# The second FFN's output product by one level of Strassen's algorithm

## The chip, the cores and the metric

The kernel runs on one core of one Trainium2 chip. The metric is device time in microseconds (us) of one execution; the profile is one execution taken by the hardware profiler, and its times are counted from the start of its span.

## The reference

One layer on 512 tokens of width 1024: a SwiGLU FFN, a mixing part (a gated linear recurrence and a forgetting attention), and a second SwiGLU FFN, each with a modulated norm ahead and a gated residual behind. Only the second FFN matters here:

```
u = rms_norm(x, ffn2_norm_g) * (1 + sc3) + sh3
a, b = jnp.split(u @ w_in, 2, axis=-1)          # w_in: 1024 x 5632
x = x + 0.5 * g3 * ((jax.nn.silu(a) * b) @ w_out)   # w_out: 2816 x 1024
```

All tensors are float32.

## The kernel before

Every product in float32 is made of three matmuls on split operands (`mm3`, L108 to L110): each operand is the sum of a high part in the format fp32r and a low part of the same format, and high times high, low times high and high times low are summed in PSUM. A weight block comes by a DMA of 512 KB issued on SP into `raw` (3 buffers), ScalarE (ACT) copies it to the high part `wh` (L89), VectorE (DVE) subtracts to get the low part `wl` (L91); `wh` and `wl` have 4 buffers each.

The hidden width 2816 is 22 blocks of 128 rows. The input product of the second FFN (`ffn_in_halves` for the first two blocks, `ffn_in` for the others) keeps the hidden values h transposed, with 128 rows of h on the partitions and 512 tokens along the free dimension. `ffn_h` makes h of a block from its two PSUM banks (`g`): ACT's silu (L324), DVE's product (L325), then the split into `hh` (L326, ACT) and `hl` (L327, DVE).

The output product is `token_gemm`, called twice, for the left and the right 512 columns of the output: in each call the 22 blocks of `w_out` are loaded in pairs (`w_mov`), and for each of the 4 blocks of 128 tokens there is one PSUM bank, in which 22 x 3 matmuls are summed. The banks of the first call are those of pool `t`, of the second those of pool `g` (4 banks each, 8 in all). The last two pairs (`tail`) are taken token block by token block, so that `residual` can finish one bank while the next is summed: DVE scales it with the gate (L388), adds x (L390), SP stores it (L394). x stays in the tiles `x0` to `x7` all the time.

The order of the instructions on each engine is set by the framework's scheduler, from the program's order and from its own estimate of the times. The engines take their instructions in that order, and semaphores hold an instruction until its inputs and its buffer are there. The wait for a buffer is a wait for its last reader.

Of the kernel before, what the change touches and what calls it, by code (L numbers as in the profile page):

```python
# [11 lines left out]
F32 = mybir.dt.float32  # L12
F32R = mybir.dt.float32r
I32 = mybir.dt.int32
AF = mybir.ActivationFunctionType
# [5 lines left out]
P = 128  # L21
T = 512
NT = 4
D = 1024
NK = 8
FF = 2816
NJ = 22
# [16 lines left out]
MUL, ADD, SUB, MAX, MIN = ALU.mult, ALU.add, ALU.subtract, ALU.max, ALU.min  # L44


class Layer:
# [285 lines left out]
    def ffn_in(self, w_in, j0, hp, tp, extra=None):  # L333
        for j in range(j0, NJ):
            pa, pb = self.gbank(), self.gbank()
            self.gemm_stat(pa, self.w_stat(w_in, j * P), 0, T)
            self.gemm_stat(pb, self.w_stat(w_in, FF + j * P), 0, T)
            self.ffn_h(pa, pb, j, 0, T, hp, tp)
            self.lo_after = None
            if extra:  # L340
                extra(j)

    def ffn_in_halves(self, w_in, nj, hp, tp):

        wa = [self.w_stat(w_in, j * P) for j in range(nj)]
        wb = [self.w_stat(w_in, FF + j * P) for j in range(nj)]
        pp = [(self.gbank(), self.gbank()) for _ in range(nj)]
        for h in range(2):
            for j in range(nj):
                c0, c1 = h * 256, (h + 1) * 256  # L350
                self.gemm_stat(pp[j][0], wa[j], c0, c1)
                self.gemm_stat(pp[j][1], wb[j], c0, c1)
                self.ffn_h(pp[j][0], pp[j][1], j, c0, c1, hp, tp)

    def token_gemm(self, lhs, nk, w, half, done, tail=2, extra=None, last=None):

# [565 lines left out]
    def run(self):  # L922
        nc, tc, A = self.nc, self.tc, self.A
# [5 lines left out]
        self.ntmp, self.xn_tiles = 5, self.xn_start  # L929
        with tc.tile_pool(name="f1t", bufs=1) as tp:  # L930
            self.consts(tp)
            with tc.tile_pool(name="st", bufs=1) as st:
# [2 lines left out]
            with tc.tile_pool(name="f1h", bufs=1) as hp:  # L935
# [12 lines left out]
                lhs = lambda k: (self.hh[k], self.hl[k])  # L948
# [25 lines left out]
        with tc.tile_pool(name="gates", bufs=1) as mp:  # L974
            ws = [self.w_stat(w_mix, m * P) for m in range(4)]
            pp = [self.gbank() for _ in range(4)]
# [6 lines left out]
            for m in range(4, 8):  # L983
                ps = self.gbank()
# [5 lines left out]
        with tc.tile_pool(name="att", bufs=1) as ip:  # L990
# [60 lines left out]
        with tc.tile_pool(name="br", bufs=1) as bp:  # L1051
# [12 lines left out]
            for m in range(NK):  # L1064
                t = self.branch(m, 1, bp, None)
# [5 lines left out]
            lhs = lambda k: (self.mh[k], self.ml[k])  # L1071
# [5 lines left out]
            self.norm_half(1, bp, G3, sh3)  # L1077
        ys.close()

        self.ntmp = 5  # L1080
        with tc.tile_pool(name="f2t", bufs=1) as tp, tc.tile_pool(name="f2h", bufs=1) as hp:
            for k in range(NK):
                self.dump(f"u3_{k}", self.uh[k].bitcast(F32))
            self.h_tiles(hp)
            self.ffn_in_halves(A["ffn2_w_in"][0], 2, hp, tp)
            self.ffn_in(A["ffn2_w_in"][0], 2, hp, tp)
            lhs = lambda k: (self.hh[k], self.hl[k])
# [32 lines left out]
```

## Time and profile before

| | |
|---|---|
| time, median of 3 runs | 1366.77 us (1366.6 to 1367.23) |
| profiled execution: time, span | 1367.67 us, 1365.9 us |
| PE (TensorE) busy | 1344.3 us, 98% of the span, 6586 matmuls |
| DVE busy | 800.8 us, 59% |
| ACT busy | 561.2 us, 41% |
| POOL (GpSimd) busy | 46.0 us, 3% |
| DMA | 183.36 MB, mean 134 GB/s |
| granted TensorE clock, mean | 0.999 |

How to read the rows: a row of the timeline gives start, duration, engine, line of the kernel, operation, out<-in, and in brackets how long the engine had been idle and what released it. A row of the waits gives the waiting engine and line, the one waited for, the sum, the number and the longest of the waits. A row of the windows gives for a stretch its length and each engine's busy time with the number of instructions, then the granted clock, the DMA engines' share and GB/s. A matmul's duration in the trace is its latency; the next one starts earlier.

### The profile page before, as it was taken

To read this page: it belongs to the slowest core of one execution; us is meant where nothing else is said; L and a number is where in the kernel's file an instruction comes from. 1 tells how busy PE (TensorE), PEld (TensorE's weight loads), DVE (VectorE), ACT (ScalarE), POOL (GpSimd) and SP (SyncE) were. 2 spreads that over 40 slices of the span, in tenths; PEclk is the share of its full clock that TensorE was granted. 3 is DMA by queue.
4 is the path that set the end of the run, shared out by engine and by line. 5 is a ranking of instruction groups with operands and counts; after the bars stand their busy time and mean duration, and the time that the engine had idled before them with its cause. 6 is when DMAs were issued, how large, how long until landed. Compare 5 with 4: busy or idle time off the path is not lost.

```text
span 1365.9 us, 17443 instructions
## 1 busy us (share of the span) xinstructions
PE 1344.3 (98%) x6586; PEld 1126.1 (82%) x6586; DVE 800.8 (59%) x1476; ACT 561.2 (41%) x945; POOL 46.0 (3%) x71
## 2 busy tenths in 40 slices
PE   7999999999999999999999999999999999999998
PEld 6788887887888888888888888888798888888887
DVE  6866666656467777886786875456473333332232
ACT  4532333323236655465665675332262223222120
POOL 2000000000011101000000000012010000000000
PEclk9999999999999999999999999999999999999999
DMA  9676556666534424434252532464323333333230
GB/s 290 185 220 191 180 181 198 215 205 193 184 89 112 117 93 135 127 104 132 63 148 72 162 109 70 132 193 147 92 79 108 94 106 94 93 96 105 101 123 31
DMA packets 216456, 183.36 MB, mean 134 GB/s; under 512 B 10866, under 2 KB 182546, under 8 KB 216372
## 3 DMA queue, kind: packets, MB, share of 16 engines
q1 hardware_dynamic: 215892, 182.17, 44.6%
q8 instruction: 52, 0.85, 0.3%
q14 instruction: 32, 0.26, 0.1%
q0 software_dynamic: 416, 0.06, 0.0%
q10 hardware_dynamic: 64, 0.02, 0.0%
HBM read 172.18 MB, written 10.03 MB: 133 GB/s over the span
## 4 chain that ended last, share of the span: by engine, by line
PE 89%; DVE 6%; ACT 3%; DMA 1%; issue 1%; SPq 0%; DVEq 0%; ACTq 0%
PE g L110 23%; PE g L108 23%; PE g L109 23%; PE t L110 4%; PE t L109 4%; PE t L108 4%; PE g L510 2%; PE t L854 2%; PE t L824 1%; DVE wl L91 1%; PE t L795 1%; PE t L796 1%; PE t L510 1%; DVE fq L774 1%; DMA A<-A_d 1%
## 5 line engine op out<-in xcount | busy, mean ns | idle before, releaser
L91 DVE TENSOR_TENSOR wl<-raw,wh 128x1024 fp32r<-128x1024 f32 x214 | 269.4, 1260 | 272.6 <-ACT wh L89 255.7
L89 ACT ACTIVATE wh<-raw 128x1024 fp32r<-128x1024 f32 x214 | 225.8, 1060 | 493.7 <-PE g L109 150.8
L110 PE MATMUL g<-uh,wl 128*128 128x512 f32 (+2 forms) x984 | 369.7, 376 | 1.8 <-DVE wl L91 1.8
L108 PE MATMUL g<-uh,wh 128*128 128x512 f32 (+2 forms) x984 | 370.7, 377 | 0.0
L109 PE MATMUL g<-ul,wh 128*128 128x512 f32 (+2 forms) x984 | 369.7, 376 | 0.0
L110 PEld LDWEIGHTS g<-uh,wl 128*128 128x128 f32 (+1 forms) x984 | 184.7, 188 | 36.4 <-DVE wl L91 2.7
L109 PEld LDWEIGHTS g<-ul,wh 128*128 128x128 f32 (+1 forms) x984 | 184.9, 188 | 33.5
L108 PEld LDWEIGHTS g<-uh,wh 128*128 128x128 f32 (+1 forms) x984 | 184.8, 188 | 33.5 <-issue 0.6
L108 PE MATMUL g<-wh,uh 128*128 128x512 f32 (+1 forms) x320 | 111.8, 350 | 0.0
L110 PE MATMUL g<-wh,ul 128*128 128x512 f32 (+1 forms) x320 | 111.1, 347 | 0.0
L109 PE MATMUL g<-wl,uh 128*128 128x512 f32 (+1 forms) x320 | 110.9, 347 | 0.0
L325 DVE TENSOR_TENSOR sl<-g,sl 128x512 f32<-128x512 f32 (+1 forms) x45 | 29.9, 667 | 82.8 <-PE g L110 82.7
L284 DVE SCALAR_TENSOR_TENSOR acc<-raw,ccol,acc 128x1024 f32<-128x1024 f32 x49 | 62.9, 1283 | 14.5 <-DMA raw<-in_w_ada_dram 14.0
L108 PE MATMUL g<-wh,hh 128*128 128x512 f32 x176 | 69.2, 393 | 0.0
L110 PE MATMUL g<-wh,hl 128*128 128x512 f32 x176 | 69.1, 393 | 0.0
L108 PE MATMUL t<-wh,hh 128*128 128x512 f32 x176 | 69.1, 392 | 0.0
L110 PE MATMUL t<-wh,hl 128*128 128x512 f32 x176 | 69.1, 392 | 0.0
L109 PE MATMUL g<-wl,hh 128*128 128x512 f32 x176 | 69.0, 392 | 0.0
L109 PE MATMUL t<-wl,hh 128*128 128x512 f32 x176 | 69.0, 392 | 0.0
L108 PEld LDWEIGHTS g<-wh,uh 128*128 128x128 f32 x320 | 60.5, 189 | 7.8 <-DVE tk L709 0.5
L110 PEld LDWEIGHTS g<-wh,ul 128*128 128x128 f32 x320 | 60.5, 189 | 7.7
L109 PEld LDWEIGHTS g<-wl,uh 128*128 128x128 f32 x320 | 60.5, 189 | 7.4
(268 smaller groups left out, 1851.5 us busy)
## 6 DMA issues: line engine op xcount, KB each, us to landing
raw<-in_ffn_w_in_dram SPq DMA_DIRECT2D x82, 512.0 KB
raw<-in_w_ada_dram SPq DMA_DIRECT2D x56, 512.0 KB
raw<-in_w_mix_dram SPq DMA_DIRECT2D x48, 512.0 KB
raw<-in_ffn_w_out_dram SPq DMA_DIRECT2D x44, 512.0 KB
ar<-in_w_ada_dram SPq DMA_DIRECT2D x32, 256.0 KB
raw<-in_w_mix_dram SPq DMA_DIRECT2D x32, 256.0 KB
A<-A_d SPq DMA_DIRECT2D x16, 256.0 KB
raw<-in_w_branch_a_dram SPq DMA_DIRECT2D x8, 512.0 KB
```

The lines of the kernel that those rows point to most:

```text
L89: nc.scalar.activation(hi, src, AF.Copy)
L91: nc.vector.tensor_tensor(lo, src, hi, op=SUB)
L108: mm(ps, lh, rh, start=start, stop=False)
L109: mm(ps, lh, rl, start=False, stop=False)
L110: self.last_mm = mm(ps, ll, rh, start=False, stop=stop)
L284: nc.vector.scalar_tensor_tensor(acc, r, self.ccol[:, k:k + 1], acc, op0=MUL, op1=ADD)
L325: nc.vector.tensor_tensor(s[:, :w], ps_b[:, c0:c1], s[:, :w], op=MUL)
L510: mm = nc.tensor.matmul(acc_ps[b], (wl if p == 1 else wh)[:, b % 2, s], self.ul[k] if p == 2 else self.uh[k], start=k == 0 and p == 0, sto ...
L774: nc.vector.scalar_tensor_tensor(lo, b[own, :], gc[own, :], d[own, :], op0=MUL, op1=SUB)
L795: nc.tensor.matmul(ps[:, :w], q[:, s], k[:, :w], start=True, stop=False)
L796: nc.tensor.matmul(ps[:, :w], q[:, s], kl[:, :w], start=False, stop=True)
L854: nc.tensor.matmul(po[:, q0:], vt[:, kb, i, :], Px[:, o:o + T - q0], start=n == 1, stop=n == 8)
```

## The change

The output product is a 512 x 2816 by 2816 x 1024 product. Split in two in each direction, with the even and the odd blocks of h as the two halves of the inner dimension, it is eight products of half size (256 tokens, 11 blocks, 512 columns); Strassen's algorithm (in Winograd's form, with sums that are used again) makes it of seven, whose operands are sums and differences of the quarters of h and of `w_out`. The new function `pair_out` does it in two sweeps over `w_out`: the first sums three products in six banks (Z, X, Y for two token blocks each), 18 matmuls per pair of blocks; the second sums four (Z, Y, X, W) in eight banks, 24 matmuls per pair. A step is one pair; steps 0 to 10 of the second sweep are written 0' to 10' here.

- `pair_h` takes the place of `ffn_h`: the product silu(a) * b of an even block goes to `E`, of an odd one to `Ra`; when both are there, DVE makes the sums of the pair (L381, L382, L385, L386). The operands of the first sweep are split at once (ACT L383, DVE L384), the others stay unsplit in `Ra` and `Rb`. The first four pairs' `Ra` and `Rb` lie in the tiles of x; x is written to DRAM ahead of the second FFN (L1254, 8 stores of 256 KB) and read back in the second sweep.
- `pair_split` splits `Ra` and `Rb` of a pair: two copies on ACT (L405), two subtractions on DVE (L406).
- Per step of the first sweep, `load` fetches the two blocks of a pair (512 KB and 256 KB); DVE makes two differences of quarters of `w_out` (L440, L441), the split of the block of 1024 columns as before (L89, L91), and a split of one more half (L423 on ACT, L424 on DVE). The second difference is kept in `T2` for the second sweep.
- Between the sweeps the sums P1, U2, U4 leave the banks (ACT L452, DVE L454, L456).
- Per step of the second sweep, the two blocks are loaded again, POOL makes two differences (L473, L474), and three splits follow (L89 and L91; L479 and L480 twice).
- In steps 6' and 7' P1, U2 and U4 are scaled (DVE L463) and added to x on POOL (L465): six scalings and eight additions. The tail, steps 9' and 10', is taken bank by bank; the first six banks' additions to x are on POOL, the others on DVE.

```diff
-            self.ffn_h(pa, pb, j, 0, T, hp, tp)
+            self.ffn_act(pa, pb, j, 0, T, hp, tp)
...
+    def pair_h(self, ps_a, ps_b, j, c0, c1, hp, tp):
...
+        V(E[:, 1, :], E[:, 3, :], Ra[:, 1, :], op=ADD)
+        V(E[:, 2, :], E[:, 1, :], E[:, 0, :], op=SUB)
+        nc.scalar.activation(A1[:, 0:3, :], E[:, 0:3, :], AF.Copy)
+        V(A1[:, 3:6, :], E[:, 0:3, :], A1[:, 0:3, :], op=SUB)
+        V(Rb[:, 0, :], E[:, 0, :], E[:, 3, :], op=SUB)
+        V(Rb[:, 1, :], Ra[:, 0, :], E[:, 2, :], op=SUB)
...
+    def pair_split(self, i, hp, tp):
...
+        for n, R in enumerate((self.Ra[i], self.Rb[i])):
+            hi = A2[:, 2 * n:2 * n + 2, :]
+            nc.scalar.activation(hi, R, AF.Copy)
+            nc.vector.tensor_tensor(lo[n], R, hi, op=SUB)
...
+    def pair_out(self, w, v, hp, tp, x_src):
...
+        def load(r, c):
+            t = self.raw([P, 2, 512], [(lambda t: t, w[r * P:(r + 1) * P, :].rearrange("p (h n) -> p h n", h=2))])
+            o = tp.tile([P, 512], F32, name=self.nm("raw2"), tag="t2", bufs=self.ntmp)
+            nc.sync.dma_start(o, w[c * P:(c + 1) * P, 512:])
+            return t, o
+        for i in range(NP):
+            t, o = load(2 * i, 2 * i + 1)
...
+            V.tensor_tensor(t[:, 1, :], t[:, 1, :], t[:, 0, :], op=SUB)
+            V.tensor_tensor(T2[i], o, t[:, 1, :], op=SUB)
+            wh, wl = self.split(t, [P, 2, 512])
+            w2 = half(T2[i])
+            A1 = self.A1[i]
+            for ps, n, b in ((Z, 0, (wh[:, 0, :], wl[:, 0, :])), (X, 2, w2), (Y, 1, (wh[:, 1, :], wl[:, 1, :]))):
+                for tb in range(2):
+                    mm(ps, tb, (A1[:, n, :], A1[:, 3 + n, :]), b, i == 0, i == NP - 1)
+            if i % 2:
+                self.pair_split(i // 2, hp, tp)
...
+        def add(src, half, tbs, eng=V):
+            t = self.tmp(tp, "rs")
+            V.scalar_tensor_tensor(t, src, 0.5, g[half], op0=MUL, op1=MUL)
+            for tb in tbs:
+                eng.tensor_tensor(self.x[tb][half], self.x[tb][half], t, op=ADD)
...
+        def prepare(i):
+            if i >= NP // 2:
+                self.pair_split(i, hp, tp)
+            t, o = load(2 * i + 1, 2 * i)
+            G.tensor_tensor(o, t[:, 1, :], o, op=SUB)
+            G.tensor_tensor(T2[i], t[:, 0, :], T2[i], op=SUB)
+            wh, wl = self.split(t, [P, 2, 512])
...
+            for n, src in enumerate((o, T2[i])):
+                nc.scalar.activation(hi[:, n, :], src, AF.Copy)
+                V.tensor_tensor(lo[:, n, :], src, hi[:, n, :], op=SUB)
...
+        for i in range(NP - tail):
+            o = prepare(i)
+            for n in ("WZXY" if i == 0 else "ZYXW"):
+                for tb in range(2):
+                    step(n, tb, i, o)
+            if i == 4:
+                self.x_tiles()
+                x_src()
+            if i in (6, 7):
+                tb = i - 6
+                add(P1[tb], 0, (tb,), G)
+                add(U2[tb], 0, (tb + 2,), G)
+                add(U4[tb], 1, (tb, tb + 2), G)
...
-        self.ntmp = 5
+        self.ntmp, self.ffn_act = 3, self.pair_h
...
-            self.token_gemm(lhs, NJ, A["ffn2_w_out"][0], 0, self.residual(0.5, 8, 0, tp, True))
-            self.token_gemm(lhs, NJ, A["ffn2_w_out"][0], 1, self.residual(0.5, 8, 1, tp, True))
+            self.pair_out(A["ffn2_w_out"][0], 8, hp, tp, lambda: self.x_load(x3))
```

Up to the second FFN each engine's instructions and their order are those of before. Three places show what the scheduler made of the rest.

DVE in the output product before: in the middle of the first call to `token_gemm`, the low parts of the weight blocks are all there is.

```order
L91 TENSOR_TENSOR wl_10943<-raw_10940,wh_10942 128x1024
L91 TENSOR_TENSOR wl_10973<-raw_10970,wh_10972 128x1024
L91 TENSOR_TENSOR wl_11003<-raw_11000,wh_11002 128x1024
L91 TENSOR_TENSOR wl_11033<-raw_11030,wh_11032 128x1024
L91 TENSOR_TENSOR wl_11063<-raw_11060,wh_11062 128x1024
```

DVE now, from the low part of step 9's weights to step 0' of the second sweep (`wl` of L91 and L424: steps 9 and 10 of the first sweep, of L91 and L480: step 0'; `Ra` and `Rb` of L406: low parts of pairs 5 to 8):

```order
L91 TENSOR_TENSOR wl_11148<-raw_11140,wh_11147 128x1024
L424 TENSOR_TENSOR wl_11152<-T_1987_11144,wh_11151 128x512
L406 TENSOR_TENSOR Rb_11455<-Rb_10102,A_2056_11453 128x512
L406 TENSOR_TENSOR Ra_11501<-Ra_10241,A_2065_11500 128x512
L406 TENSOR_TENSOR Rb_11502<-Rb_10242,A_2065_11500 128x512
L406 TENSOR_TENSOR Ra_11558<-Ra_10381,A_2077_11557 128x512
L91 TENSOR_TENSOR wl_11188<-raw_11180,wh_11187 128x1024
L424 TENSOR_TENSOR wl_11192<-T_1997_11184,wh_11191 128x512
L406 TENSOR_TENSOR Rb_11559<-Rb_10382,A_2077_11557 128x512
L406 TENSOR_TENSOR Ra_11615<-Ra_10521,A_2089_11614 128x512
L406 TENSOR_TENSOR Rb_11616<-Rb_10522,A_2089_11614 128x512
L91 TENSOR_TENSOR wl_11244<-raw_11237,wh_11243 128x1024
```

The scheduler has moved the splits of pairs 5 to 8, which the program has in steps 5' to 8', ahead of the end of the first sweep: 18 of the 22 subtractions of L406 stand before the first weights of the second sweep.

POOL has nothing in the output product before; its last instructions belong to the norm ahead of the second FFN:

```order
L247 TENSOR_TENSOR ul_8971<-uf_9124,uh_8963 128x256
L247 TENSOR_TENSOR ul_8973<-uf_9132,uh_8965 128x256
L247 TENSOR_TENSOR ul_8975<-uf_9140,uh_8967 128x256
L247 TENSOR_TENSOR ul_8977<-uf_9148,uh_8969 128x256
L1116 UNCONDITIONAL_BRANCH
```

POOL now, from the differences of step 6' to those of step 8' (`raw` of L473 and `T` of L474: differences of the weights; `x` of L465: the additions to x):

```order
L473 TENSOR_TENSOR raw_2069_11509<-raw_11507,raw_2069_11509 128x512
L465 TENSOR_TENSOR x_11437<-x_11437,rs_11547 128x512
L474 TENSOR_TENSOR T_1970_11071<-raw_11564,T_1970_11071 128x512
L465 TENSOR_TENSOR x_11438<-x_11438,rs_11553 128x512
L465 TENSOR_TENSOR x_11442<-x_11442,rs_11553 128x512
L474 TENSOR_TENSOR T_1980_11111<-raw_11621,T_1980_11111 128x512
L465 TENSOR_TENSOR x_11441<-x_11441,rs_11550 128x512
L465 TENSOR_TENSOR x_11439<-x_11439,rs_11604 128x512
L473 TENSOR_TENSOR raw_2081_11566<-raw_11564,raw_2081_11566 128x512
L474 TENSOR_TENSOR T_1987_11144<-raw_11668,T_1987_11144 128x512
L465 TENSOR_TENSOR x_11440<-x_11440,rs_11610 128x512
L465 TENSOR_TENSOR x_11443<-x_11443,rs_11607 128x512
```

The eight additions to x (the eighth, to `x_11444`, follows the last row) stand between the differences of steps 6' and 8', and step 7' gets its second difference (the ninth row) behind five of them.

More of the change, by code (lines that the diff above doesn't have):

```diff
@@ L352, in ffn_in_halves @@
                 self.gemm_stat(pp[j][1], wb[j], c0, c1)
-                self.ffn_h(pp[j][0], pp[j][1], j, c0, c1, hp, tp)
+                self.ffn_act(pp[j][0], pp[j][1], j, c0, c1, hp, tp)
+    def pair_h(self, ps_a, ps_b, j, c0, c1, hp, tp):
+        nc = self.nc
+        i, w, h0 = j // 2, c1 - c0, c0 // 256
+        nh = w // 256
+        s = self.tmp(tp, "sl")
+        nc.scalar.activation(s[:, :w], ps_a[:, c0:c1], AF.Silu)
+        hv = lambda t: t.rearrange("p (h t) -> p h t", t=256)
+        if j % 2 == 0:
+            if h0 == 0:
+                self.E = tp.tile([P, 4, 256], F32, name=self.nm("E"), tag="E", bufs=2)
+            nc.vector.tensor_tensor(self.E[:, 0:4:3, :] if nh == 2 else self.E[:, 3 * h0:3 * h0 + 1, :],
+                                    hv(ps_b[:, c0:c1]), hv(s[:, :w]), op=MUL)
+            return
+        if h0 == 0:
+            self.Ra[i], self.Rb[i] = self.pair_rest(i, hp, F32)
+        Ra, Rb = self.Ra[i], self.Rb[i]
+        nc.vector.tensor_tensor(Ra[:, h0:h0 + nh, :], hv(ps_b[:, c0:c1]), hv(s[:, :w]), op=MUL)
+        if c1 < T:
+            return
+        E, V = self.E, nc.vector.tensor_tensor
+        A1 = self.A1[i] = hp.tile([P, 6, 256], F32R, name=self.nm("A1"), tag=f"A{i}", bufs=1)
+        V(E[:, 1, :], E[:, 3, :], Ra[:, 1, :], op=ADD)
[4 more added lines that the diff above has]
+        V(Rb[:, 1, :], Ra[:, 0, :], E[:, 2, :], op=SUB)
@@ new lines, in pair_rest @@
+    def pair_rest(self, i, hp, dt):
+        new = (lambda n, x: self.xp.tile([P, 2, 256], dt, name=self.nm(n), tag=f"x{2 * i + x}")) if i < 4 else \
+            (lambda n, x: hp.tile([P, 2, 256], dt, name=self.nm(n), tag=f"{n}{i}", bufs=1))
+        return new("Ra", 0), new("Rb", 1)
+    def pair_split(self, i, hp, tp):
+        nc = self.nc
+        A2 = hp.tile([P, 4, 256], F32R, name=self.nm("A2"), tag=f"A{i}", bufs=1)
+        if i:
+            lo = self.pair_rest(i - 1, hp, F32R)
+        else:
+            t = tp.tile([P, 4, 256], F32R, name=self.nm("Rl"), tag="E", bufs=2)
+            lo = t[:, 0:2, :], t[:, 2:4, :]
+        for n, R in enumerate((self.Ra[i], self.Rb[i])):
+            hi = A2[:, 2 * n:2 * n + 2, :]
+            nc.scalar.activation(hi, R, AF.Copy)
+            nc.vector.tensor_tensor(lo[n], R, hi, op=SUB)
+        self.A2[i] = A2, *lo
@@ new lines, in pair_out, with half, mm, store @@
+    def pair_out(self, w, v, hp, tp, x_src):
+        nc = self.nc
+        V, G = nc.vector, nc.gpsimd
+        slots = iter([f"{a}{k}" for k in range(NK) for a in ("uh", "ul")])
+        new = lambda n, dt=F32: self.up.tile([P, 512], dt, name=self.nm(n), tag=next(slots))
+        early = tp.tile([P, 2, 512], F32, name=self.nm("T2"), tag="E", bufs=2)
+        NP = NJ // 2
+        T2 = [early[:, 0, :], early[:, 1, :]]
+        Z, Y = [[self.tbank() for _ in range(2)] for _ in range(2)]
+        X = [self.gbank() for _ in range(2)]
+        def half(src):
+            hi = self.wp.tile([P, 512], F32R, name=self.nm("wh"), tag="wh", bufs=4)
+            lo = self.wp.tile([P, 512], F32R, name=self.nm("wl"), tag="wl", bufs=4)
+            nc.scalar.activation(hi, src, AF.Copy)
+            V.tensor_tensor(lo, src, hi, op=SUB)
+            return hi, lo
+        def mm(ps, tb, a, b, start, stop):
+            s = slice(tb * P, (tb + 1) * P)
+            self.mm3(ps[tb], a[0][:, s], a[1][:, s], b[0], b[1], start, stop)
+        def load(r, c):
[5 more added lines that the diff above has]
+            t, o = load(2 * i, 2 * i + 1)
+            if i >= 2:
+                T2.append(new("T2"))
+            V.tensor_tensor(t[:, 1, :], t[:, 1, :], t[:, 0, :], op=SUB)
[8 more added lines that the diff above has]
+                self.pair_split(i // 2, hp, tp)
+        P1, U2, U4 = [[new(n) for _ in range(2)] for n in ("P1", "U2", "U4")]
+        for tb in range(2):
+            nc.scalar.activation(P1[tb], Z[tb], AF.Copy)
+        for tb in range(2):
+            V.tensor_tensor(U2[tb], X[tb], P1[tb], op=ADD)
+        for tb in range(2):
+            V.tensor_tensor(U4[tb], Y[tb], U2[tb], op=ADD)
+        W, X = [[self.gbank() for _ in range(2)] for _ in range(2)]
+        Z, Y = [[self.tbank() for _ in range(2)] for _ in range(2)]
+        g = [self.mod_bcast(v, 0, tp), new("gb")]
+        nc.sync.dma_start(g[1], self.mod_d[v:v + 1, 512:].to_broadcast([P, 512]))
+        def add(src, half, tbs, eng=V):
[3 more added lines that the diff above has]
+                eng.tensor_tensor(self.x[tb][half], self.x[tb][half], t, op=ADD)
+        def store(tb, half):
+            nc.sync.dma_start(self.out[0, tb * P:(tb + 1) * P, half * 512:(half + 1) * 512], self.x[tb][half])
+        def prepare(i):
[5 more added lines that the diff above has]
+            wh, wl = self.split(t, [P, 2, 512])
+            hi = self.wp.tile([P, 2, 512], F32R, name=self.nm("wh"), tag="wh", bufs=4)
+            lo = self.wp.tile([P, 2, 512], F32R, name=self.nm("wl"), tag="wl", bufs=4)
+            for n, src in enumerate((o, T2[i])):
+                nc.scalar.activation(hi[:, n, :], src, AF.Copy)
+                V.tensor_tensor(lo[:, n, :], src, hi[:, n, :], op=SUB)
+            A2 = self.A2[i]
+            a = lambda n: (A2[0][:, n, :], A2[1 + n // 2][:, n % 2, :])
+            b = lambda n: ((wh, hi)[n // 2][:, n % 2, :], (wl, lo)[n // 2][:, n % 2, :])
+            return {"Z": (a(0), b(0)), "Y": (a(3), b(1)), "X": (a(2), b(2)), "W": (a(1), b(3))}
+        banks = {"Z": Z, "Y": Y, "X": X, "W": W}
+        step = lambda n, tb, i, o: mm(banks[n], tb, *o[n], i == 0, i == NP - 1)
+        tail = 2
+        for i in range(NP - tail):
+            o = prepare(i)
+            for n in ("WZXY" if i == 0 else "ZYXW"):
+                for tb in range(2):
+                    step(n, tb, i, o)
[7 more added lines that the diff above has]
+                add(U4[tb], 1, (tb, tb + 2), G)
+        os = [prepare(i) for i in range(NP - tail, NP)]
+        for n in "ZYXW":
+            for tb in range(2):
+                for i, o in enumerate(os):
+                    step(n, tb, NP - tail + i, o)
+                ps = banks[n][tb]
+                if n == "Z":
+                    add(ps, 0, (tb,), G)
+                    store(tb, 0)
+                elif n == "Y":
+                    add(ps, 1, (tb,), G)
+                    store(tb, 1)
+                elif n == "X":
+                    add(ps, 1, (tb + 2,), G)
+                    store(tb + 2, 1)
+                    add(ps, 0, (tb + 2,))
+                else:
+                    add(ps, 0, (tb + 2,))
+                    store(tb + 2, 0)
@@ L1078, in run @@
         ys.close()
-        self.ntmp = 5
+        self.ntmp, self.ffn_act = 3, self.pair_h
+        self.A1, self.A2, self.Ra, self.Rb = [[None] * (NJ // 2) for _ in range(4)]
         with tc.tile_pool(name="f2t", bufs=1) as tp, tc.tile_pool(name="f2h", bufs=1) as hp:
@@ L1083, in run @@
                 self.dump(f"u3_{k}", self.uh[k].bitcast(F32))
-            self.h_tiles(hp)
+            x3 = self.dp.tile([T, D], F32, name="x3_d")
+            for tb in range(NT):
+                for h in range(2):
+                    nc.sync.dma_start(x3[tb * P:(tb + 1) * P, h * 512:(h + 1) * 512], self.x[tb][h])
             self.ffn_in_halves(A["ffn2_w_in"][0], 2, hp, tp)
             self.ffn_in(A["ffn2_w_in"][0], 2, hp, tp)
-            lhs = lambda k: (self.hh[k], self.hl[k])
-            self.token_gemm(lhs, NJ, A["ffn2_w_out"][0], 0, self.residual(0.5, 8, 0, tp, True))
-            self.token_gemm(lhs, NJ, A["ffn2_w_out"][0], 1, self.residual(0.5, 8, 1, tp, True))
+            self.pair_out(A["ffn2_w_out"][0], 8, hp, tp, lambda: self.x_load(x3))
 _INS = ["x", "c", "w_ada", "b_ada", "ffn1_norm_g", "ffn1_w_in", "ffn1_w_out", "mix_norm_g", "w_mix", "b_mix",
```

2 lines of the change are left out of this document (1 added, 1 removed).

## The prediction

> **What bounds the kernel now.** I read the page first, then the windows, the timeline and the waits of the second FFN. The page has PE busy nearly all the time; the windows say the same of the output product alone, and the timeline gives its first and its last matmul.
>
> ```profile
> PE 1344.3 (98%) x6586; PEld 1126.1 (82%) x6586; DVE 800.8 (59%) x1476; ACT 561.2 (41%) x945; POOL 46.0 (3%) x71
> ...
> 1241.50:1361.20 119.70, 119.63 (x528) 98.74 (x526) 34.04 (x36) 20.51 (x20) 0.00 (x0) 1.00 0.26 88
> ...
> 1241.29 0.39 PE L108 MATMUL t<-wh,hh 128*128 128x512 f32 x1
> ...
> 1360.90 0.24 PE g L110
> 1361.14 0.02 issue
> 1361.17 0.70 DVE rs L388
> 1361.87 0.02 issue
> 1361.89 0.69 DVE x L390
> ```
>
> 528 matmuls, PE busy without a gap, 34 us of DVE in 120. From the first start to the last (1360.90 in the chain of waits) are 119.61 us in 527 intervals: 0.227 us per matmul. Behind the last one stand a scaling, an addition (to 1362.58) and a store. So PE alone sets this stage, and every matmul left out is worth 0.227 us as long as the operands come in time. The waits show how early they come:
>
> ```profile
> DVE wl L91 <- ACT wh L89: 105.0, 37, 4.2
> ```
>
> DVE waits before nearly every low part (37 times, 105 us from 1140 on), for ACT, which itself waits for PE to free a buffer: both are ahead of PE by the depth of the buffers.
>
> **What is removed.** 528 matmuls become 7 products x 2 token blocks x 11 pairs x 3 = 462. 66 x 0.227 = 15.0 us less on PE, on the path. That is the whole gain, about 1.1%.
>
> **What is added, and where it lies.** From the last input matmul on, DVE gets far more to do. Its prices (L463 is here a line of before, a low part of another width; 128x256 is priced at 0.33):
>
> ```profile
> L91 DVE TENSOR_TENSOR wl<-raw,wh 128x1024 fp32r<-128x1024 f32 x214 | 269.4, 1260 | 272.6 <-ACT wh L89 255.7 <-PE g L109 9.5 <-PE t L109 4.4
> L463 DVE TENSOR_TENSOR wl<-raw,wh 128x768 fp32r<-128x768 f32 x7 | 6.7, 952 | 0.0
> 903.04 3.70 DVE L918 TENSOR_TENSOR yl<-yb,yh 128x512 fp32r<-128x512 f32 x6
> ...
> 1302.80 1.22 DVE L91 TENSOR_TENSOR wl<-raw,wh 128x1024 fp32r<-128x1024 f32 x1
> 1303.94 0.68 DVE L390 TENSOR_TENSOR x<-x,rs 128x512 f32<-128x512 f32 x1
> ```
>
> In a full queue a 128x512 subtraction (0.69 us alone) follows the next after (3.70 - 0.69) / 5 = 0.60 us, and one of 128x1024 takes 1303.94 - 1302.80 = 1.14. DVE's order from the last product of h to the low part of the last weights (step 10') has 20 of 128x1024, 80 of 128x512 (22 L406, 20 L480, 17 L440 and L441, 10 L424, 6 L463, 4 L454 and L456, one product), one of 128x768 and three of 128x256: 22.8 + 48.0 + 0.9 + 1.0 = 72.7 us. PE's time over the same piece is 11 x 18 + 9 x 24 + 4 = 418 matmuls, 94.9 us. DVE alone would fit, though barely in the first sweep: 1.14 + 5 x 0.60 = 4.1 us per step (L91, L424, L440, L441, two L406) against 18 x 0.227 = 4.1.
>
> But POOL works beside it now, and before's trace has POOL beside DVE at eight places, in the branch part. Two of them, DVE and POOL rows in order of time:
>
> ```profile
> 912.88 1.23 DVE L91 TENSOR_TENSOR wl<-raw,wh 128x1024 fp32r<-128x1024 f32 x1 [0.17 <-ACT wh L89]
> 912.93 2.33 POOL L1066 TENSOR_TENSOR sg<-sg,ta 128x512 f32<-128x512 f32 x1 [382.44 <-DMA raw<-in_w_branch_b_dram]
> 918.34 1.30 POOL L1066 TENSOR_TENSOR sg<-sg,ta 128x512 f32<-128x512 f32 x1 [3.07 <-ACT wh L89]
> 918.38 2.35 DVE L91 TENSOR_TENSOR wl<-raw,wh 128x1024 fp32r<-128x1024 f32 x1 [0.17 <-ACT wh L89]
> ```
>
> The one that starts second stretches by about the length of the other: POOL's addition from 1.30 to 2.33, DVE's subtraction from 1.23 to 2.35. They do not share, they take turns, and a POOL operation of 128x512 costs DVE 2.35 - 1.23 = 1.12 us. POOL has 2 per step of the second sweep and 8 additions to x; 29 of them stand ahead of step 10's weights (10 L473, 11 L474, 8 L465): 29 x 1.12 = 32.5 us. Together 72.7 + 32.5 = 105.2. Five DVE instructions of the piece (L454, L456, the product) read PSUM and one tile of SBUF, and such a one was not held up:
>
> ```profile
> 1010.41 0.85 POOL L247 TENSOR_TENSOR ul<-uf,uh 128x256 fp32r<-128x256 f32 x1 [9.69 <-DVE uf L246]
> 1010.58 1.00 DVE L246 TENSOR_SCALAR uf<-t,G,sh 128x256 f32<-128x256 f32 x2
> ```
>
> (two of 0.54 in 1.00). So 3.0 us of the sum may overlap: 102.2 to 105.2, against 94.9 on PE. Steps in which DVE waits (for POOL to give back the buffer that a scaling L463 needs: three times a few tenths) add about 0.5. That is a deficit of 7.8 to 10.8 us; I take 9. **PE waits for it**, in two places. At the end of the first sweep DVE owes 42.2 us (10 of 128x1024, 48 of 128x512, the rest) and POOL already 4 or 5 operations for 0' and 1', against 44.9 of PE: 2 to 3 us. In steps 6' to 9' POOL's eight additions and six scalings put 9.0 + 3.6 us on top of 1.14 + 1.20 + 2.24 = 4.6 per step of 5.45: about 6 us. In between DVE gains 0.9 per step, but no more than the two spare buffers hold.
>
> The Trainium skill has the rule (SBUF — State Buffer, "Who interferes with whom"): a VectorE instruction with two inputs in SBUF and a GpSimd instruction that reads SBUF exclude each other, and the second waits for the whole of the first. The rows agree in kind. By the whole of POOL's 1.30 us instead of 1.12 the estimate would be 29 x 0.18 = 5.2 us more, 1367.6, no change; the second rival below is this rule carried to DVE's side too.
>
> **At the end** six banks' additions are on POOL, 1.30 us each, one per bank of 6 x 0.227 = 1.36 us, so POOL keeps pace with nothing to spare; the scaling of bank W waits for a buffer that POOL's last addition frees, and three DVE additions of 0.6 to 0.7 queue behind. I count to the last addition about 3.0 us from the last matmul, where before it was 1362.58 - 1361.14 = 1.4: 1.6 us more, between 0 (buffer free in time) and 3 (two POOL operations late).
>
> **Edits that cost nothing.** The sums in `pair_h` lie beside the input product:
>
> ```profile
> 1152.00:1241.00 89.00, 89.00 (x394) 73.73 (x393) 29.95 (x32) 25.23 (x32) 0.00 (x0) 1.00 0.33 100
> ```
>
> DVE is busy 30 us of 89 there, and a pair gains five small operations, some 2.4 us in 21.8; without that cover it would be those 2.4 per pair. ACT in the output product gets 1.06 + 4 x 0.63 at most per step of 4.1 us, two thirds. DMA: 768 KB per step are 193 GB/s in the first sweep and 144 in the second, where the page's row by slices has 290 at most; a load lands some 3.7 us after its issue:
>
> ```profile
> 357.65 0.33 SPq L79 DMA_DIRECT2D raw<-in_w_ada_dram  x1
> 361.39 1.28 DVE L284 SCALAR_TENSOR_TENSOR acc<-raw,ccol,acc 128x1024 f32<-128x1024 f32 x1 [2.64 <-DMA raw<-in_w_ada_dram]
> ```
>
> With three buffers a load is issued two steps ahead of its use. The eight stores of x stand on SP among the first loads of the input product, whose weights for the third block are needed some 20 us later; x comes back when steps 1' to 4' have freed its tiles, and behind those waits on SP stand only loads for step 6' and later. If a load came late, one step would slip by 1 to 2 us.
>
> **The sum**, against the profiled execution: 1367.67 - 15.0 + 9.0 + 1.6 = 1363.3. The median of the runs shown lies 0.9 below that execution, so 1362.4.
>
> **Rivals.**
> - POOL costs DVE little here: its operations fall into DVE's pauses. For it speaks that DVE's own 72.7 us leave 22 free; against it that in both sweeps DVE's next instruction stands ready, and that it was held up in all seven cases where POOL started first. Then PE waits 1 us at most and the tail stays: -15.0 + 1.0 + 1.6, 1354.4.
> - The other side: DVE and POOL take turns at their full durations, 1.26 and 0.69 and 1.30, because a blocked instruction cannot start its overhead early. Then 20 x 1.26 + 80 x 0.69 + 2.3 + 29 x 1.30 = 120.4 against 94.9: 25.5 us of waiting at PE, 1366.8 - 15.0 + 25.5 + 1.6 = 1378.9. It is slower than before from a sum of 94.9 + 13.4 = 108.3 us on, 4.4 us above mine (103.9). Against it: the two rows at 912.88 end 2.38 us apart from the start of both, where their durations alone add up to 2.53. Halfway, some 1370, is the likelier form.
> - PE falls to half speed after its waits. The clock column shows 1.00 throughout, but the same transpose takes 5.33 / 24 = 0.22 us after 6.6 us of idle and 1.91 / 16 = 0.12 later:
>
> ```profile
> 6.83 5.33 PE L483 MATMUL t<-ident 128*128 128x128 f32 x24
> 22.23 1.91 PE L518 MATMUL t<-ident 128*128 128x128 f32 x16
> 25.88 1.19 PE L510 MATMUL g<-uh,wh 128*128 128x512 f32 x4 [1.41 <-ACT uh L475]
> ```
>
>   After 1.41 us of idle four matmuls take 1.19, so that one does not trigger it. My waits are 0.5 to 3 us each; if three of them did, at some 2.5 us each (half of those first 5), 1370.
>
> **How the numbers follow.** A measurement of this kernel can tell 0.2%, 2.7 us, from no change: faster ends at 1364.0, slower begins at 1369.5. My forecast 0.45 (its own range 1358 to 1368; faster 0.30, same 0.15), no contention 0.22 (faster), full durations 0.20 (slower), half speed 0.13 (same 0.05, slower 0.08). Faster 0.52, same 0.20, slower 0.28. The range leaves out half of the first rival and the far part of the second: 1354 to 1372.
>
> **What would show it.** In the profile after: 462 matmuls at 0.227 us in the output product; rows of L480, L91 and L406 stretched by some 1.1 us where a POOL row overlaps, none of L454 and L456; PE waiting for `wl` of L91, L424 or L480 at the end of the first sweep and in steps 6' to 9', 9 us in sum; the last addition 3 us behind the last matmul. It would be wrong if PE waits for a DMA or for ACT, if DVE is idle where PE waits, or if PE waits in the middle of the first sweep.

## The result, and the profile after

The changed kernel takes 1366.17 us (median of 12 runs, 1364.83 to 1369.53) where the kernel before takes 1366.92 (12 runs, 1366.6 to 1367.84) beside it: ratio 0.9998, 95% interval 0.9989 to 1.0006. Run again later (11 runs against 15) it was 0.9984, 0.9976 to 0.9993. By the medians it is 0.75 and 1.5 us faster; the first interval includes a ratio of 1, the second just leaves it out. The forecast was 1362.4 with a range of 1354 to 1372, and "faster" was its likeliest case: the time lies in the range, 3.8 us above the forecast, and the gain that was forecast (4.4 us) did not come.

The profiled execution after took 1364.83 us, its span is 1362.6. The row of the engines on its page:

```profile
PE 1332.7 (98%) x6520; PEld 1114.1 (82%) x6520; DVE 887.8 (65%) x1592; ACT 589.4 (43%) x989; POOL 109.8 (8%) x107
```

66 matmuls fewer, 87 us more of DVE, 64 more of POOL. The waits from the output product on (us in total, times, longest):

```profile
DVE rs L463 <- POOL x L465: 7.0, 3, 4.9
...
PE t L109 <- DVE wl L91: 6.2, 3, 2.9
...
DVE wl L480 <- ACT wh L479: 1.8, 1, 1.8
...
PE g L109 <- DVE wl L480: 1.8, 2, 1.1
```

PE, which waited nowhere in this stage before, waits 8.0 us, every time for a low part that DVE writes. The timeline has the first matmul of the stage, the five waits, the last matmul, and DVE's last addition:

```profile
1240.17 0.39 PE L108 MATMUL t<-wh,A 128*128 128x512 f32 x1
...
1286.62 0.50 PE L109 MATMUL g<-wl,A 128*128 128x512 f32 x1 [1.08 <-DVE wl L480]
...
1299.26 0.50 PE L109 MATMUL t<-wl,A 128*128 128x512 f32 x1 [1.46 <-DVE wl L91]
...
1324.76 0.50 PE L109 MATMUL g<-wl,A 128*128 128x512 f32 x1 [0.69 <-DVE wl L480]
...
1330.98 0.50 PE L109 MATMUL t<-wl,A 128*128 128x512 f32 x1 [2.86 <-DVE wl L91]
...
1346.30 0.50 PE L109 MATMUL t<-wl,A 128*128 128x512 f32 x1 [1.86 <-DVE wl L91]
...
1356.18 0.39 PE L110 MATMUL g<-wh,Ra 128*128 128x512 f32 x1
...
1358.96 0.69 DVE L465 TENSOR_TENSOR x<-x,rs 128x512 f32<-128x512 f32 x1
```

The waits lie at the sweep boundary (step 0'), in step 2', in 6' and 7', and in the tail for step 10'. In before the first and the last matmul of the stage start at 1241.29 and 1360.74, which is 527 intervals of 0.2267 us; by that, the 461 intervals after would take 104.5 and take 116.0. So PE loses 11.5 us: the 8.0 of the waits, 2.2 at half speed (shown below), and the rest at the start behind each wait. From first matmul to the end of the span the stage takes 122.4 us after and 124.6 before: **2.2 us less, -15.0 + 11.5 + 1.3**, where the last 1.3 is the longer way from the last matmul to the end. The other 1.1 us between the two spans lie ahead of this stage and do not count: nearly all of it is there already at the start of the kernel, which the change does not touch (the same matmul starts at 24.00 us before and at 23.02 after).

How DVE loses its time, rows of DVE and POOL from the timeline:

```profile
1274.38 7.72 POOL L473 TENSOR_TENSOR raw<-raw,raw 128x512 f32<-128x512 f32 x1 [260.50 <-ACT A L405]
...
1299.13 1.77 DVE L480 TENSOR_TENSOR wl<-raw,wh 128x512 fp32r<-128x512 f32 x1
1300.83 0.68 DVE L480 TENSOR_TENSOR wl<-T,wh 128x512 fp32r<-128x512 f32 x1
...
1312.64 1.76 DVE L463 SCALAR_TENSOR_TENSOR rs<-U,gb 128x512 f32<-128x512 f32 x1 [1.45 <-POOL x L465]
1323.41 0.69 DVE L463 SCALAR_TENSOR_TENSOR rs<-P,gb 128x512 f32<-128x512 f32 x1 [4.93 <-POOL x L465]
...
1346.77 0.68 DVE L480 TENSOR_TENSOR wl<-T,wh 128x512 fp32r<-128x512 f32 x1
```

A low part of 128x512 takes 0.68 us alone and 1.77 behind a POOL operation: 1.09 us for one turn. And the two scalings stand idle for 1.45 and 4.93 us, because POOL's additions have not given back the buffers that the scalings write. I call **the chain** the time from the stage's first matmul to the end of the last low part (the last row): 1240.17 to 1347.45, 107.3 us.

Behind the 2.86 us wait PE also ran at half speed. The windows of 2 us, PE alone (busy time and matmuls, granted clock, DMA):

```profile
1331.00:1333.00 2.00, 2.00 (x6) 0.69 0.00 0
1333.00:1335.00 2.00, 2.00 (x6) 0.50 0.10 29
```

### The profile page after: what moved, and what is told of

The parts are those of the page before. It is cut to its first block, busy times and chain, and to the rows that moved or that the text cites. A ratio compares the mean times of both kernels' runs of the same rounds, so it can differ in the third digit from the quotient of the medians.

```text
span 1362.6 us, 17660 instructions
## 1 busy us (share of the span) xinstructions
PE 1332.7 (98%) x6520; PEld 1114.1 (82%) x6520; DVE 887.8 (65%) x1592; ACT 589.4 (43%) x989; POOL 109.8 (8%) x107
## 4 chain that ended last, share of the span: by engine, by line
PE 81%; DVE 10%; ACT 3%; issue 2%; DMA 2%; POOL 1%; POOLq 0%; SPq 0%; DVEq 0%; ACTq 0%
PE g L110 22%; PE g L108 21%; PE g L109 21%; PE t L109 3%; PE t L110 3%; PE t L108 3%; DVE wl L91 2%; PE g L676 2%; PE t L1020 2%; DVE wl L480 1%; PE t L990 1%; POOL x L465 1%; PE t L961 1%; PE t L962 1%; PE t L676 1%
## 5 line engine op out<-in xcount | busy, mean ns | idle before, releaser
L89 ACT ACTIVATE wh<-raw 128x1024 fp32r<-128x1024 f32 x214 | 225.9, 1060 | 411.4 <-PE g L109 141.3
L91 DVE TENSOR_TENSOR wl<-raw,wh 128x1024 fp32r<-128x1024 f32 x214 | 275.0, 1286 | 180.4 <-ACT wh L89 161.1
L108 PE MATMUL g<-yh,wh 128*128 128x512 f32 x128 | 50.4, 394 | 0.0
L110 PE MATMUL g<-yh,wl 128*128 128x512 f32 x128 | 50.2, 392 | 0.0
L109 PE MATMUL g<-yl,wh 128*128 128x512 f32 x128 | 49.7, 388 | 0.0
L247 POOL TENSOR_TENSOR ul<-uf,uh 128x256 fp32r<-128x256 f32 x16 | 13.4, 837 | 448.7 <-DVE uf L246 448.7
L473 POOL TENSOR_TENSOR raw<-raw,raw 128x512 f32<-128x512 f32 x11 | 25.1, 2281 | 262.0 <-ACT A L405 260.5
L1232 POOL TENSOR_TENSOR sg<-sg,ta 128x512 f32<-128x512 f32 x8 | 11.4, 1425 | 412.2 <-DMA raw<-in_w_branch_b_dram 383.9
L972 ACT ACTIVATE S<-S,mn 128x128 f32<-128x128 f32 (+1 forms) x64 | 35.6, 558 | 18.7 <-DVE mn L964 9.7
```

What stands on the lines that cost most here:

```text
L89: nc.scalar.activation(hi, src, AF.Copy)
L91: nc.vector.tensor_tensor(lo, src, hi, op=SUB)
L108: mm(ps, lh, rh, start=start, stop=False)
L109: mm(ps, lh, rl, start=False, stop=False)
L110: self.last_mm = mm(ps, ll, rh, start=False, stop=stop)
L473: G.tensor_tensor(o, t[:, 1, :], o, op=SUB)
```

## The experiments

Theories: **A**, the amount of work: DVE's own work and POOL's turns make a chain longer than PE's work, and the chain sets the end. **B**, the buffers: the waits of steps 6' to 10' come from DVE's idle time for the buffers that POOL holds. **C**, the clock: the half speed behind the waits is what eats the gain. Ratios are to the kernel before in the same set of runs.

**Scalings in place.**

```
-            t = self.tmp(tp, "rs")
+            t = t or self.tmp(tp, "rs")
...
-                add(P1[tb], 0, (tb,), G)
+                add(P1[tb], 0, (tb,), G, P1[tb])     # U2 and U4 likewise
```

> The six scalings L463 of steps 6' and 7' write their result over their source (P1, U2, U4), so none of them needs one of the three t2 buffers; the additions stay on POOL, nothing else changes. Theory A (amount): PE waits because DVE's work and POOL's turns at the SBUF port sum to more than PE's time; the work is the same, so PE's waits of steps 6' to 10' (0.7 + 2.9 + 1.9 us) only shift, and the time stays within 1 us of 1366.2. Theory B (buffers): those waits come from DVE standing idle 7.0 us for buffers that POOL's additions hold; the idle goes, the 2.9 us wait and the half-speed stretch behind it (1.9 us) go with it, PE's waits in the output product fall from 8.0 to 4.5 us or less, and the time falls by 4 to 5.5 us, to about 1361.

1365.05 us, ratio 0.9981 (0.9972 to 0.9989). A row of the waits, and two groups of DVE:

```profile
DVE rs L463 <- POOL x L465: 0.6, 1, 0.6
```
```profile
L91 DVE TENSOR_TENSOR wl<-raw,wh 128x1024 fp32r<-128x1024 f32 x20 | 32.4, 1622 | 0.4 <-ACT wh L89 0.3
L480 DVE TENSOR_TENSOR wl<-raw,wh 128x512 fp32r<-128x512 f32 x11 | 16.2, 1471 | 0.3 <-ACT wh L479 0.3
```

The buffers' idle time went from 7.0 to 0.6 us, and the chain shrank only from 107.3 to 105.9. What the idle gave, the turns took. I sum DVE's rows from the last product of h to the last low part: the time by which rows are longer than the same operation alone, that is the turns, grew from 23.5 to 30.1 us (L480 on `raw` from a mean of 1261 to 1471 ns), and the idle time fell from 8.8 to 0.9. While DVE stood idle, POOL had worked through its operations for nothing. B is good for 1.4 us on the chain and no more; A holds, though the median fell by 1.1 us where it allowed 1. PE waits 6.7 us, with a stretch at half speed behind one wait.

**Differences on DVE.**

```
-            G.tensor_tensor(o, t[:, 1, :], o, op=SUB)
-            G.tensor_tensor(T2[i], t[:, 0, :], T2[i], op=SUB)
+            V.tensor_tensor(o, t[:, 1, :], o, op=SUB)
+            V.tensor_tensor(T2[i], t[:, 0, :], T2[i], op=SUB)
```

> The 22 differences of the second sweep (L473, L474) go from POOL to DVE; POOL keeps the additions to x. Theory A: each costs DVE 0.60 us in a full queue in place of 1.12 us at the port, 22 x 0.52 = 11.4 us less before step 10'; the waits at the boundary and in step 2' (1.1 and 1.5 us) go and so do most of the later ones, PE waits 1 to 2 us in all, the half-speed stretch goes: 1357 to 1359. Theory B: the boundary waits go, but the scalings still wait for buffers that the additions hold (shorter, since no difference stands between them): PE waits 3 to 4 us in steps 6' to 8': 1362 to 1364. Against both: a difference that waits on DVE for its load or for the matmuls that read T holds up the low parts queued behind it; then PE waits where it did not before.

1356.78 us, ratio 0.9921 (0.9907 to 0.9934). Giving DVE 22 operations *more* takes 9 us off the changed kernel. All of PE's waits and one of DVE's, and the last low part in the timeline:

```profile
PE t L109 <- DVE wl L91: 2.7, 2, 1.7
...
DVE raw L473 <- DMA raw<-in_ffn_w_out_dram: 1.8, 3, 1.1
```
```profile
1339.53 0.68 DVE L480 TENSOR_TENSOR wl<-T,wh 128x512 fp32r<-128x512 f32 x1
```

The waits at the boundary and in step 2' are gone, as A said. The chain (from 1240.86) is 99.4 us, 7.9 less where 22 x 0.52 = 11.4 was expected. By DVE's rows its own work grew by 13.4 us, the turns fell by 16.1 and its idle time by 5.2: together 21.3 for 22 operations, 0.97 each, not 1.12. Part of the idle time left is the case "against both": differences now wait on DVE for their loads (1.8 us), and low parts queue behind them.

**All on DVE**: the two edits above together, and every addition's `G` a `V`.

> Differences and all additions on DVE, early scalings in place: POOL does nothing in the output product. Theory A: DVE's sum up to step 10' is 72.7 + 30 x 0.60 = 90.7 us against 94.9 of PE; it fits, PE waits less than 1 us, the tail ends about 2 us behind the last matmul: 1366.9 - 15.0 + 1 + 0.5, about 1353. Rival (order): DVE takes its instructions in a fixed order with only 4 us to spare, and stands idle where the next one waits for a load or for ACT, so PE still waits 4 to 6 us: 1358 to 1360.

1354.61 us, ratio 0.9903 (0.9888 to 0.9918): faster than both kernels, 13.1 us below before in the same set, where 13.5 was expected. PE has no wait left; the timeline's last low part, last matmul and last additions, and then DVE's largest group:

```profile
1336.80 0.68 DVE L480 TENSOR_TENSOR wl<-T,wh 128x512 fp32r<-128x512 f32 x1
...
1345.93 0.39 PE L110 MATMUL g<-wh,Ra 128*128 128x512 f32 x1
...
1348.71 1.28 DVE L465 TENSOR_TENSOR x<-x,rs 128x512 f32<-128x512 f32 x2
```
```profile
L91 DVE TENSOR_TENSOR wl<-raw,wh 128x1024 fp32r<-128x1024 f32 x20 | 24.3, 1217 | 1.9 <-ACT wh L89 1.8
```

L91's mean is the lone 1217 ns: without POOL nothing stretches. The stage's first matmul starts at 1241.44 here, and 1345.93 - 1241.44 = 104.5 us, 461 intervals without a loss, where 1 us was allowed. The tail is longer than expected: 4.1 us from the last matmul's start to the last addition's end, 2.2 more than before, where 0.5 was allowed.

**Zero matmuls in the waits.**

```
+            for _ in range(k):     # k = 5 ahead of step 2', 10 of 7', 6 of 10'
+                nc.tensor.matmul(banks["Z"][0], zero, some, start=False, stop=False)
```

> The changed kernel with 21 matmuls of zero weights (they add nothing) that fill three of PE's waits: 5 ahead of step 2', 10 ahead of step 7', 6 ahead of step 10' in the tail (0.227 us each; the waits there are 1.5, 2.9 and 1.9 us). The operands come no earlier. Theory C (clock): after its longest wait PE runs some 9 matmuls at half speed; with the wait filled the granted clock stays at 1.00, the profiled span is 1.9 us shorter, and the median of the runs falls by 2 to 3 us and their spread (1364.8 to 1369.5) shrinks to about 1 us. Rival: the lower clock has nothing to do with the waits: no change of the median beyond 0.5 us and the same spread.

1366.03 us, ratio 0.9988 (0.998 to 0.9997); the runs spread from 1364.88 to 1368.06. PE in step 7' and the last low part (timeline; L482 is the line of L480 here), and the clock behind that wait (windows):

```profile
1328.43 2.45 PE L493 MATMUL t<-A,zero 128*128 128x512 f32 x10
...
1331.70 0.50 PE L109 MATMUL t<-wl,A 128*128 128x512 f32 x1 [0.59 <-DVE wl L91]
...
1347.65 0.68 DVE L482 TENSOR_TENSOR wl<-T,wh 128x512 fp32r<-128x512 f32 x1
```
```profile
1332.00:1334.00 2.00, 2.00 (x10) 1.00 0.00 0
```

The wait was filled and the clock stayed at 1.00, and nothing was won: from the first matmul (1240.90) the chain takes 107.4 us, as before the filling. The half speed is real and its cause is the wait, but here it costs nothing, since PE only arrives at the next wait later. C falls as the account of the lost gain. The spread, 3.2 us, did not shrink to 1 either.

**The changed kernel again**, unaltered.

> The changed kernel once more, unaltered, for a second profile and for a comparison in the same conditions as the others here. Theory A (the chain of DVE and POOL from the last product of h to the low part of step 10's weights sets the end): that chain again takes 107 us (107.3 in the first profile, 107.4 with the zero matmuls), whatever PE's clock does behind its waits, and the stage from its first matmul to the end of the span again takes 122.4 us, 2.2 us less than before's 124.6; the ratio is 0.998 to 1.000. Theory C (clock): stage and ratio vary with the stretches at half speed; a run with two such stretches has a stage 2 us longer.

1365.67 us, ratio 0.9984 (0.9976 to 0.9993). Its profile happens to repeat the test of C. Two of PE's waits and the last low part (timeline), and the windows behind the first wait:

```profile
1331.51 0.80 PE L109 MATMUL t<-wl,A 128*128 128x512 f32 x1 [2.86 <-DVE wl L91]
...
1346.82 0.50 PE L109 MATMUL t<-wl,A 128*128 128x512 f32 x1 [0.64 <-DVE wl L91]
...
1347.29 0.68 DVE L480 TENSOR_TENSOR wl<-T,wh 128x512 fp32r<-128x512 f32 x1
```
```profile
1330.00:1332.00 2.00, 0.49 (x1) 0.68 0.00 0
1332.00:1334.00 2.00, 2.00 (x6) 0.50 0.00 0
1334.00:1336.00 2.00, 2.00 (x7) 0.50 0.32 81
1336.00:1338.00 2.00, 2.00 (x7) 0.61 0.53 180
```

Behind the same 2.86 us wait PE was at half speed for twice as long, and the next wait shrank from 1.86 to 0.64 us. The chain (from 1240.72) is 107.2 us, the stage 122.4, as in the first profile.

**The eight early additions on DVE**: in steps 6' and 7', `G` becomes `V`.

> Only the eight additions to x of steps 6' and 7' go from POOL to DVE; the 22 differences stay on POOL, the scalings keep the t2 buffers, the tail is unaltered. Theory A: 8 x (1.12 - 0.60) = 4.2 us less on the chain, and DVE no longer stands idle for POOL to give back buffers (7.0 us, of which the in-place run got back 1.4 on the chain): the chain takes 101 to 103 us in place of 107, the time falls by 4 to 6 us against the changed kernel, to about 1361. If POOL's operations cost DVE nothing, the eight additions on DVE cost 8 x 0.60 = 4.8 us more: 1370.

1360.93 us, ratio 0.9947 (0.9933 to 0.9961), 4.7 us by the medians (0.0037, or 5.1 us, by the ratios) below the changed kernel in the same set: A's number. The last low part, from a first matmul at 1242.38:

```profile
1344.58 0.68 DVE L480 TENSOR_TENSOR wl<-T,wh 128x512 fp32r<-128x512 f32 x1
```

The chain is 102.9 us, 4.4 less: by DVE's rows 4.9 us more of its own work, 5.6 less of turns and 3.8 less of idle time, so 1.17 for each operation that left POOL.

**Another order of the tail**, on top of all on DVE:

```
-        for n in "ZYXW":
+        for n in "ZXYW":     # Z, and the half 1 of X, on POOL; Y, and the half 0 of X and W, on DVE
```

> As the run with all on DVE, with the last product's banks in the order Z, X, Y, W in place of Z, Y, X, W, and four of the tail's ten additions (Z, and the half 1 of X) on POOL, where DVE works on scalings, which read PSUM. In the run with all on DVE the last addition ends 3.8 us behind the last matmul, because DVE has 20 operations of 0.60 us, 12.0 us, against 10.9 of PE, and the bank with four of them comes third. Theory (tail): with 16 on DVE and the four of X earlier, the last addition ends 1.4 to 2 us behind the last matmul: 2 us less, 1352.6. Rival: POOL's additions take turns with DVE's additions, and the scalings wait for buffers that POOL holds: no change, 1354.6.

1353.88 us, ratio 0.9896 (0.9883 to 0.991), the lowest of all; its interval overlaps that of all on DVE, so the two are not told apart. The tail in DVE's and PE's rows:

```profile
1341.31 1.06 DVE L465 TENSOR_TENSOR x<-x,rs 128x512 f32<-128x512 f32 x1
...
1343.55 0.69 DVE L463 SCALAR_TENSOR_TENSOR rs<-t,gb 128x512 f32<-128x512 f32 x1 [0.58 <-POOL x L465]
...
1345.64 0.39 PE L110 MATMUL g<-wh,Ra 128*128 128x512 f32 x1
...
1348.48 0.69 DVE L465 TENSOR_TENSOR x<-x,rs 128x512 f32<-128x512 f32 x1
```

From the last matmul's start to the last addition's end are 3.5 us, 0.5 less than with all on DVE, where 2 were expected. The rival's two losses are both in the rows: an addition stretched by 0.4 us, a scaling held 0.58 for POOL's buffer.

**Waits of known length**, in the kernel before, where PE is the bound:

```
+            n = self.times.get(self.count, 1)      # 13 to 18 at eight places, 1 elsewhere
-            nc.vector.tensor_tensor(lo, src, hi, op=SUB)
+            for _ in range(n):
+                r = nc.vector.tensor_tensor(lo, src, hi, op=SUB)
```

> The kernel before, in whose second FFN eight low parts L91 are computed 13 to 18 times over (same result), 30 us or more apart, so that PE waits eight times, by my count between 0 and 5 us, each wait by itself with PE busy before and after. It costs the sum of the waits, some 20 us, and tells when the granted clock halves. C1: what decides is the length of the wait; all above about 2.3 us are followed by some 3.4 us at half speed (as after the 2.9 us wait of the changed kernel), none below. C2: the length alone does not decide (in the in-place run a wait of 2.5 us had no such stretch and one of 2.3 us had): between 2 and 4 us some waits are followed by it and some are not; above 6.8 us all.

1413.09 us (one run), 46 more than before, not 20. All eight places gave a wait, from 1.10 to 7.40 us. Four of them (timeline) and the clock behind the second row's (windows of 1 us):

```profile
1089.72 0.52 PE L116 MATMUL g<-uh,wl 128*128 128x512 f32 x1 [2.37 <-DVE wl L96]
...
1127.86 0.79 PE L116 MATMUL g<-uh,wl 128*128 128x512 f32 x1 [3.62 <-DVE wl L96]
...
1308.13 0.50 PE L115 MATMUL t<-wl,hh 128*128 128x512 f32 x1 [1.61 <-DVE wl L96]
...
1361.08 0.79 PE L115 MATMUL g<-wl,hh 128*128 128x512 f32 x1 [3.67 <-DVE wl L96]
```
```profile
1128.00:1129.00 1.00, 1.00 (x3) 0.50 0.08 22
...
1130.00:1131.00 1.00, 1.00 (x3) 0.50 1.03 301
1131.00:1132.00 1.00, 1.00 (x6) 0.99 0.88 248
```

The eight waits sum to 30.8 us. Another 12.2 us are half speed: 59 matmuls that waited for nothing start later than 0.227 us after the one before, by that much in sum. So where PE is the bound, half speed costs time, about 2 us behind each of the six waits that had it. These are the waits of 2.37 us and more; those of 1.10 and 1.61 had none. In this run the length divides them, as C1 has it, but not together with the in-place run: there a wait of 2.25 us had the stretch and one of 2.54 had not, which is C2. The last section shows what decides.

## Why the prediction was right in kind and wrong in size

- **Removed, 15.0 us: right.** 462 matmuls, 461 intervals of 0.2267 us where PE does not wait. (The last matmul of before starts at 1360.74; the 1360.90 of the prediction is a piece of the chain. The price per matmul stays.)
- **The turns: right in price.** 1.77 - 0.68 = 1.09 us against 1.12 predicted; stretched rows of L480, L91 and L463 and one of L406, and none of L454 and L456 (677 and 678 ns). The rule of the Trainium skill (SBUF — State Buffer, "Who interferes with whom"), by which the second waits for the whole of the first, agrees with the rows in kind; one turn by them is 1.09, not POOL's full 1.30. Over the whole chain turns and idle time come to about 1 us for each POOL operation: 1.17 by the eight additions that were moved, 0.97 by the 22 differences.
- **The sum of DVE and POOL, 103.9 us against PE's 94.9: the step that failed.** To the low part L91 of step 10' it was 1346.24 - 1240.37 = 105.9, and PE lost 11.5 us, not 9.0. Two terms in it were mis-sized in opposite directions. DVE's idle time was put at 0.5 ("three times a few tenths"); it was 8.8. Of that, 6.4 are the two scalings that waited for POOL, above all the 4.93 us for POOL's last addition of step 6', and 1.8 a wait for ACT, which waited for POOL in its turn. The turns were put at about 31 (32.5 less what reads PSUM) and were 23.5, because POOL's operations cost nothing while DVE stands idle: 23 stretched rows for 30 POOL operations (29 in the prediction). DVE's own work was 73.6 where 72.7 was counted. So it is in part luck that the sum came within 2 us. The in-place run shows how the two terms belong together: with the idle time at 0.6 the turns are 30.1, and the sum to the same low part is 104.1, close to the forecast's 103.9. What the prediction lacked is the wait for the buffers, less what POOL got done in it.
- **Where PE waits: partly.** 2 to 3 us at the boundary and 6 in steps 6' to 9' were forecast: 1.08 and 1.46 came in steps 0' and 2', 3.55 in 6' and 7', and 1.86 in the tail. That DVE would be idle where PE waits was named as what would prove the argument wrong. During the five waits themselves DVE's rows have no idle time; it lies ahead of them (the longest ends at 1323.41, and PE's next wait begins at 1324.07). So the sign did not show as it was worded, but the idle time was missing from the sum all the same. PE never waited for a DMA or for ACT, nor inside the first sweep.
- **The tail, 1.6 us: right.** From the last matmul's start to the last addition's end 3.47 us after and 1.84 before; to the end of the span it is 1.3. The reason given was right too: the scaling of bank W waited 0.58 us for POOL.
- **The rivals.** "POOL costs DVE little" and "full durations" are out by the rows. "PE falls to half speed" came true once, behind the longest wait, and cost nothing in the end: it was priced as an addition to the waits, but where DVE is the bound, what PE loses by it comes off the next wait.
- The total: -15.0 + 11.5 + 1.3 = -2.2 us in the stage, 2.2 short of the -4.4 forecast. The medians say -0.75 and -1.5; what is left between these and the stage is within the spread of the runs. Its cause stays open; the two longest of the twelve runs, 1368.97 and 1369.53, are also those with the lowest mean clock, 0.995.

The gain itself was there: with POOL out of the way it is 13 us of the 15.

## What to carry to other kernels

Before work is put on an idle engine, look at what it shares with the engine that sets the pace: a POOL operation that runs for 1.30 us beside DVE cost DVE 1.09, where DVE would have done the work in 0.60. Sum the chain that feeds the bound engine with these turns in it, and try what happens if the loaded engine does everything itself; here that was worth 11 to 13 us. And a stall that disappears (idle time, half speed) buys nothing while the sum behind it stays: compare the chain from end to end, not the stalls.

## What the runs showed of the hardware

- TensorE's granted clock halves behind waits shorter than I had thought, and length alone does not decide. With a stretch of half speed: 2.25 us (in the in-place run), 2.37 (in the run with waits of known length), 2.86 (twice), and 3.6 to 7.4. Without: 1.86 and all shorter ones, but also one of 2.54 in the in-place run (its timeline, and windows for PE alone around each of the two waits):

```profile
1301.10 0.50 PE L109 MATMUL t<-wl,A 128*128 128x512 f32 x1 [2.54 <-DVE wl L91]
...
1315.95 0.50 PE L109 MATMUL t<-wl,A 128*128 128x512 f32 x1 [2.25 <-DVE wl L91]
```
```profile
1296.78:1300.19 3.41, 1.79 (x8) 1.00 0.02 7
1300.19:1303.60 3.41, 2.50 (x11) 1.00 0.44 114
...
1313.84:1317.25 3.41, 1.30 (x6) 1.00 0.16 17
1317.26:1320.67 3.41, 3.41 (x10) 0.50 0.92 308
```

  What decides can be read from where the stretches begin and end. In each of the ten profiles these times are whole multiples of 3.413 us apart (in the in-place run half speed lasts from 1317.26 to 1320.67 and comes back behind the last matmul at 1358.22, 11 x 3.413 later). The four windows above lie on this grid. The wait of 2.54 us is split by it: PE is idle for 1.62 us in one window and 0.91 in the next. Of the wait of 2.25 us, 2.11 lie in one window, and half speed begins at that window's end. So it is in all ten profiles: a window at full speed in which PE was idle for 1.98 us or more was always followed by half speed, one with 1.62 or less never, and there is none between. A half-speed window was followed by another where PE was idle for 0.77 us or more in it, and by full speed where it was 0.44 or less; so the same 2.86 us wait had one window of half speed in the first profile and two in the second, where 0.77 us of the wait reached into the first of them. No run moved a wait on purpose; the rule is read from these profiles alone. The Trainium skill (TensorE: Matmul & The Clock Gate, "Part 1: The HAM clock gate") has a free-running window of some 3.4 us. The grid of these traces agrees.
- DVE and POOL do not always take turns one for one. POOL's first difference took 7.72 us (first row of DVE and POOL above; POOL's spans are rough), and 7.56 and 7.83 in the in-place run and with the additions on DVE. In the first of these DVE had a full queue from 1274.38 to 1280.90, all of it at the spacing of a full queue (0.60 us for 128x512), and the first DVE operation behind a turn of POOL's is the one at 1280.90. With both queues full later on, they alternate. What lets POOL in was not tested.
